# Operand sums of a seven-product down-projection: two of them kept in PSUM, none on GpSimd, five banks for products

## The chip, the cores and the metric

One core of one Trainium2 chip runs the whole program. The metric is the time of one execution in microseconds (us) on the device, as the median of several executions. The engines are TensorE (PE, its weight loads PEld), VectorE (DVE), ScalarE (ACT), GpSimd (POOL) and SyncE (SP, which issues the DMAs).

## The reference

A decoder block of 1024 tokens and width 1024: two token mixers, a layer norm, a convolved gated MLP, a layer norm, a gated embedding and a last norm. The part that is changed is the down-projection of the MLP:

```python
h = causal_dwconv(x @ w_up[i], conv_w[i], conv_b[i])
h_gate, h_val = jnp.split(h, 2, axis=-1)
ffn = (jax.nn.silu(h_gate) * h_val) @ w_down[i]          # (1024 x 2816) @ (2816 x 1024)
x = layer_norm(DEEPNORM_ALPHA * x + ffn, ln2_g[i], ln2_b[i])
```

All is in float32. The kernel splits each float32 operand into a high part (rounded to the multiplier's format) and a low part (what is left), and multiplies high by high, high by low and low by high.

## The kernel before

The first 18 of the 22 row blocks of w_down (each 128 rows) are multiplied in a two-by-two block scheme with seven products in place of eight (the last four blocks follow in a plain scheme and are not touched). The work has three chunks of K (c = 0, 1, 2, six row blocks each), two column groups (cb) and two token groups (gi): twelve **steps**, in the order of `todo` (line 1164), numbered 0 to 11 here. A step is one call of `down` (line 1127): 7 products of 18 matmuls of 128x256, 126 in all, gathered in three PSUM banks: A takes products 0 and 4, B takes 1, 3 and 5, Dk takes 2 and 6. Sums on VectorE (tiles `um`) combine the banks, and four sums per step add the results to the residual `res_all` (a multiply-add by ALPHA when c is 0, line 1159; else a sum, line 1161 by `sums`, line 164).

What the products need is prepared by two functions. `wd_sets(c, cb)` (line 1114) reads 768 columns of w_down per partition into a tile `dr` (one buffer), makes the four combinations in place in it, and writes seven operands `wu` (7 buffers, one full set). `act_sets(c, gi)` (line 1098) does it for the activations, in two halves `a` of 384 columns each, from tiles `ar` (3 buffers, read back from the scratch tensor d_act) into seven operands `au` (13 buffers, two sets of seven less one). Each operand's high part is written by ScalarE (`hi_of`, line 99) and its low part by VectorE or GpSimd (`lo_of`, line 105). The strings AE, BE, SE and TE (line 1125) say which of the two does a low part (AE, BE) and a sum (SE, TE). So a weight set is 4 sums and 7 low parts of 128x768 on VectorE (3 and 5 of them) and GpSimd (1 and 2); an activation set is 8 sums and 14 low parts of 128x384 on VectorE (6 and 7) and GpSimd (2 and 7). A weight set and an activation set together are called a **pair** here; the stage has six pairs.

Before step i, `prepare` emits the sets that step i+1 needs. The order on each engine is then set by a scheduler, so an emission order is not an engine's order. A wu buffer is written again only when the matmuls of two steps have read it, and an au buffer when its steps have.

PSUM has eight banks in this stage (`psum_banks(c1, "f", ch=8)`, line 1095), all for the products: they rotate, so steps i and i+1 have three each and step i+2 two.

At the stage's start the previous stage (up-projection and convolution) still has one block to finish on VectorE, ScalarE and GpSimd (`last_conv`, line 1171, tile `cv`); its result is stored to d_act, and the residual is loaded behind that store, since it lies where those tiles lay (lines 1172 to 1183).

Of the kernel before, what the change touches and what calls it, by code (L numbers as in the profile page):

```python
# [13 lines left out]
ALU = mybir.AluOpType  # L14
# [3 lines left out]
P = 128  # L18
# [12 lines left out]
ALPHA = 2.0 ** 0.25  # L31
# [9 lines left out]
def hybrid_block(ctx: ExitStack, tc: tile.TileContext, x, p, w_in, w_gate_up, b_gate, g_gla, w_gla,  # L41
# [5 lines left out]
    x, p, out = x[0], p[0, 0], out[0]  # L47
# [18 lines left out]
    def psum_banks(stack, tag, **kw):  # L66
        for name, bufs in kw.items():
            PS[name] = pool(f"ps_{tag}_{name}", bufs, PSUM, stack)
# [21 lines left out]
    def nm(s):  # L90
        uid[0] += 1
        return f"{s}_{uid[0]}"
# [15 lines left out]
    def split(hi, lo, src, eh="A", el="V"):  # L108
        hi_of(hi, src, eh)
        lo_of(lo, src, hi, el)  # L110
# [103 lines left out]

    def quad(a):
        return a.rearrange("p (a b) -> p a b", b=P)

    def transpose_in(dst, t, src):

# [755 lines left out]
    with ExitStack() as c1:  # L975
# [101 lines left out]
        late = []  # L1077
# [14 lines left out]
        return (upool if tag == "au" else wpool).tile([P, 2, 768], F32R, name=nm(tag), tag=tag, bufs=bufs)  # L1092

    with ExitStack() as c1:
        psum_banks(c1, "f", ch=8)
        dpl = pool("dwork", stack=c1)

        def act_sets(c, gi):
            U = [unit() for _ in range(7)]
            vw = [u.rearrange("p x (k a q) -> p x k a q", k=3, a=2) for u in U]  # L1100
            acts[c, gi] = vw
            steps = []
            for a in range(2):
                raw = rawp.tile([P, 6, 256], F32, name=nm("ar"), tag="ar", bufs=3)
                t0 = (4 * gi + 2 * a) * P
                loads[0] = nc.sync.dma_start(raw, d_act[c][:, :, t0:t0 + 256])
                q = raw.rearrange("p (h k) (g q) -> p h g k q", h=2, g=2)

                def put(j, src, a=a):
                    split(vw[j][:, 0, :, a], vw[j][:, 1, :, a], src, "A", AE[a][j])  # L1110
                steps.append(left_operands(q[:, 0, 0], q[:, 1, 0], q[:, 0, 1], q[:, 1, 1], put, SE))
            return [lambda x=x, y=y: (x(), y()) for x, y in zip(*steps)]

        def wd_sets(c, cb):
            raw = rawp.tile([P, 6, 2, 256], F32, name=nm("dr"), tag="dr")
            for i in range(2):
                nc.sync.dma_start(raw[:, :, i], wdown_v[:, 6 * c:6 * c + 6, i * HALF + cb * 256:i * HALF + cb * 256 + 256])
            q = raw.rearrange("p (h k) g c -> p h g k c", h=2)
            U = [unit("wu", 7) for _ in range(7)]
            vw = [u.rearrange("p x (k c) -> p x k c", k=3) for u in U]  # L1120
            ws[c, cb] = vw
            return right_operands(q[:, 0, 0], q[:, 0, 1], q[:, 1, 0], q[:, 1, 1],
                                  lambda j, src: split(vw[j][:, 0], vw[j][:, 1], src, "A", BE[j]), TE)

        AE, BE, SE, TE = ('VGVGVGV', 'GVGVGVG'), 'VVGVVGV', 'VVGV', 'VVGV'

        def down(act, W, c, cb, gi):
            A, B, Dk = (bank("ch", (P, 2, 256)) for _ in range(3))
            cols = [slice(i * HALF + cb * 256, i * HALF + cb * 256 + 256) for i in range(2)]

            def prod(ps, j, start):
                for a in range(2):
                    for k in range(3):
                        for n, (x, y) in enumerate(((0, 0), (0, 1), (1, 0))):
                            mm(ps[:, a], act[j][:, x, k, a], W[j][:, y, k], start and a == k == n == 0,
                               k == n == 2, True)

            def tmp():
                return dpl.tile([P, 2, 256], F32, name=nm("um"), tag="um", bufs=4)
            prod(A, 0, True)  # L1140
            s1 = tmp()
            S.activation(s1, A, AF.Copy)
            prod(B, 1, True)
            u2 = tmp()
            sums(u2, s1, B, ALU.add)
            prod(Dk, 2, True)
            prod(B, 3, False)
            u3 = tmp()
            sums(u3, s1, B, ALU.add)
            sums(u3, u3, Dk, ALU.add)  # L1150
            prod(A, 4, False)
            prod(B, 5, False)
            prod(Dk, 6, False)
            sums(s1, s1, B, ALU.add)
            sums(u2, u2, Dk, ALU.add)
            for g, i, src, e in ((1, 1, u3, "V"), (0, 0, A, "V"), (1, 0, s1, "V"), (0, 1, u2, "V")):
                rv = resv[:, gi, :, g, cols[i]]
                if c == 0:
                    V.scalar_tensor_tensor(rv, rv, ALPHA, src, ALU.mult, ALU.add)
                else:  # L1160
                    sums(rv, rv, src, ALU.add, e)

        loads = [None]
        todo = [(c, cb, gi) for c in range(3) for cb in range(2) for gi in range(2)]
# [12 lines left out]
        for i, (c, cb, gi) in enumerate(todo):  # L1177
            if i + 1 < len(todo):
                prepare(*todo[i + 1])
            if i == 0:  # L1180
                with tc.issue_after(loads[0].ins):
                    for t in range(NT):
                        nc.sync.dma_start(RS["res"][t], d_x1[t])
            down(acts[c, gi], ws[c, cb], c, cb, gi)

    def act_plain(i):
        raw = wp.tile([P, 1024], F32, name=nm("wr"), tag="wr", bufs=2)
# [143 lines left out]
```

## Time and profile before

| what | value |
|---|---|
| median of 3 executions | 2160.23 us (2158.56 to 2161.76) |
| profiled execution, its own time | 2157.95 us |
| its span in the profile | 2156.2 us |
| the down-projection's seven-product stage in it | 1735.7 to 1963.5 us, 227.8 us |

The profile shows one execution. "Busy" is the time in which an engine ran an instruction; the granted clock (PEclk) is TensorE's clock as a share of full speed. In rows of the timeline, instructions of the same kind that follow each other are merged: start, length, engine, line, operation, tiles, shape, count, and in brackets the idle time before and who ended it.

### The profile page before, as it was taken

The page shows a single profiled execution, that of the slowest core. Times are in us where ns is not written, and L with a number is a line of the kernel's source. Part 1 is how long each engine was busy: PE and PEld are TensorE (multiplying, and loading weights), DVE is VectorE, ACT ScalarE, POOL GpSimd, SP SyncE. Part 2 cuts the span into 40 slices and gives each one's busy share as a digit, 9 for nine tenths or more (in the row PEclk, how much of TensorE's full clock was granted, in tenths as well). Part 3 has the DMA queues.
Part 4 walks back from the last instruction along what each step waited for, and adds up shares of the span by engine and source line. Part 5 has one row for each costly group of instructions (what it writes and reads, how often), then busy time and mean ns, then how long its engine had stood idle before and what let it go on. Part 6 is the DMA issues. An engine that isn't in the chain of part 4 may idle for free.

```text
span 2156.2 us, 32472 instructions
## 1 busy us (share of the span) xinstructions
PE 2067.9 (96%) x12210; PEld 1815.2 (84%) x12210; DVE 1585.9 (74%) x2700; ACT 841.9 (39%) x1498; POOL 996.8 (46%) x808
## 2 busy tenths in 40 slices
PE   9999999999999999999999979999999978989997
PEld 8888899998988888887788977877777768989897
DVE  3489999999227888786234587777777789986965
ACT  4343312213126766675222244434443444332421
POOL 2432443634431121213332676767767765444743
PEclk9999999999999999999999989999999989999999
DMA  4222211211226776779666351222222134223222
GB/s 137 79 64 79 86 33 55 62 45 52 74 77 126 140 153 133 141 160 227 209 198 148 129 173 49 88 79 78 79 79 88 55 124 150 89 93 118 89 98 79
DMA packets 377566, 227.14 MB, mean 105 GB/s; under 512 B 189328, under 2 KB 351760, under 8 KB 377408
## 3 DMA queue, kind: packets, MB, share of 16 engines
q1 hardware_dynamic: 377408, 225.06, 38.3%
q8 instruction: 96, 1.57, 0.3%
q14 instruction: 62, 0.51, 0.1%
HBM read 146.37 MB, written 40.89 MB: 87 GB/s over the span
## 4 chain that ended last, share of the span: by engine, by line
PE 22%; DVE 12%; POOL 8%; issue 7%; DMA 2%; ACT 2%; SPq 0%; POOLq 0%; DVEq 0%; ACTq 0%
PE mm L155 12%; PE ch L155 10%; POOL wl L106 5%; DVE au L106 2%; DVE cv L1064 1%; DVE wu L106 1%; DVE um L164 1%; DVE h L1020 1%; DVE dr L164 1%; DMA wr<-d_ob 1%; DVE ar L164 1%; ACT cv L1062 1%; DVE res_all L164 1%; POOL lnmv L212 1%; DMA dr<-in_w_down_dram 1%
## 5 line engine op out<-in xcount | busy, mean ns | idle before, releaser
L106 POOL TENSOR_TENSOR wl<-wr,wh 128x512 fp32r<-128x512 f32 x304 | 439.9, 1460 | 287.3 <-ACT wh L101 279.7
L155 PE MATMUL ch<-xs,wh 128*128 128x512 f32 x1232 | 384.8, 394 | 6.7 <-ACT wh L101 4.1
L155 PE MATMUL mm<-Ah,wh 128*128 128x512 f32 x832 | 331.6, 399 | 2.2 <-ACT wh L101 1.3
L155 PE MATMUL mm<-Al,wh 128*128 128x512 f32 x832 | 330.1, 397 | 0.3 <-POOL Al L106 0.3
L155 PE MATMUL mm<-Ah,wl 128*128 128x512 f32 x832 | 329.3, 396 | 0.0
L155 PEld LDWEIGHTS ch<-xs,wh 128*128 128x128 f32 x1232 | 231.7, 189 | 59.4 <-ACT wh L101 4.6
L103 POOL TENSOR_SCALAR wh<-wr 128x512 fp32r<-128x512 f32 x112 | 76.9, 690 | 383.2 <-PE mm L155 199.8
L155 PE MATMUL ch<-xs,wl 128*128 128x512 f32 x616 | 242.4, 394 | 6.6 <-POOL wl L106 6.5
L155 PE MATMUL ch<-wu,au 128*128 128x256 f32 x1512 | 197.1, 294 | 31.2 <-DVE um L164 14.4
L155 PEld LDWEIGHTS ch<-wu,au 128*128 128x128 f32 x1512 | 192.5, 201 | 36.0 <-DVE um L164 14.7
L155 PE MATMUL mm<-wl,Ah 128*128 128x256 f32 x768 | 217.8, 285 | 4.7 <-POOL wl L106 4.6
L155 PE MATMUL mm<-wh,Al 128*128 128x256 f32 x768 | 216.3, 284 | 0.0
L155 PE MATMUL mm<-wh,Ah 128*128 128x256 f32 x768 | 213.8, 284 | 0.0
L1064 DVE SCALAR_TENSOR_TENSOR cv<-h,cw,cv 128x1023 f32<-128x1023 f32 x88 | 167.6, 1905 | 59.9 <-ACT cv L1062 58.4
L101 ACT ACTIVATE wh<-wr 128x512 fp32r<-128x512 f32 (+1 forms) x201 | 120.6, 622 | 186.7 <-PE mm L155 77.0
L155 PEld LDWEIGHTS mm<-Ah,wh 128*128 128x128 f32 x832 | 156.3, 188 | 32.9 <-ACT wh L101 1.8
L155 PEld LDWEIGHTS mm<-Ah,wl 128*128 128x128 f32 x832 | 156.2, 188 | 32.9
L155 PEld LDWEIGHTS mm<-Al,wh 128*128 128x128 f32 x832 | 156.4, 188 | 30.5 <-POOL Al L106 0.8
L651 DVE MATCH_REPLACE8 score<-m,score 128x896 f32<-128x896 f32 (+3 forms) x192 | 166.4, 868 | 0.0
L650 DVE MAX8 m<-score 128x8 f32<-128x896 f32 (+3 forms) x192 | 163.4, 875 | 2.3 <-POOL score L457 2.1
L155 PEld LDWEIGHTS mm<-wl,Ah 128*128 128x128 f32 x768 | 145.8, 190 | 6.4 <-POOL wl L106 5.7
L106 POOL TENSOR_TENSOR wl<-ar,wh 128x512 fp32r<-128x512 f32 x77 | 127.7, 1677 | 44.9 <-ACT wh L101 44.9
(261 smaller groups left out, 4327.0 us busy)
## 6 DMA issues: line engine op xcount, KB each, us to landing
wr<-in_w_in_dram SPq DMA_DIRECT2D x60, 512.0 KB, 3.9
wr<-in_w_up_dram SPq DMA_DIRECT2D x22, 512.0 KB, 3.9
ar<-in_w_up_dram SPq DMA_DIRECT2D x22, 512.0 KB, 3.9
d_act<-cv SPq DMA_DIRECT2D x22, 512.0 KB, 2.6
dr<-in_w_down_dram SPq DMA_DIRECT2D x12, 768.0 KB, 7.1
ar<-d_act SPq DMA_DIRECT2D x12, 768.0 KB, 5.7
d_tg<-tg SPq DMA_DIRECT2D x32, 256.0 KB, 2.0
wr<-in_w_out_dram SPq DMA_DIRECT2D x16, 512.0 KB, 3.6
```

The costliest lines, as they stand in the source:

```text
L101: S.activation(dst, src, AF.Copy, scale=scale)
L103: (V if eng == "V" else G).tensor_scalar(dst, src, scale, 0.0, ALU.mult, ALU.add)
L106: done["GV"[eng != "G"]] = (G if eng == "G" else V).tensor_tensor(out=dst, in0=src, in1=hi.bitcast(F32), op=ALU.subtract)
L155: T.matmul(ps, lhsT=l, rhs=r, start=start, stop=stop, skip_group_check=more)
L164: (G if eng == "G" else V).tensor_tensor(out=out, in0=a, in1=b, op=op)
L212: G.tensor_scalar(dst, src, scale, eps, ALU.mult, ALU.add)
L650: V.max(m8, score[t])
L651: V.match_replace(score[t], m8, score[t], TAKEN)
L1020: V.tensor_tensor(out=out, in0=a, in1=quad(b), op=ALU.add)
L1062: S.activation(o, h, AF.Identity, bias=cbias[:, c:c + 1], scale=cw[:, 2, c:c + 1])
L1064: V.scalar_tensor_tensor(o[:, d:], h[:, :L - d], cw[:, 2 - d, c:c + 1], o[:, d:], ALU.mult, ALU.add)
```

## The change

A new function `bank_sets` takes the place of `left_operands` and `right_operands` in this stage. Of the four combinations of an operand, the first two (s1 = the difference of two blocks, s3 = a third block less s1) are written to two PSUM banks of a new pool `cx` (three banks), and read from there by ScalarE (high part) and VectorE (low part); the other two are still made in place in SBUF. All sums are VectorE's. Of the seven low parts three are VectorE's (the two in PSUM and one more) and four GpSimd's. Weight sets are now cut into two halves of 384 columns, like the activation sets. So each half set has 4 sums and 3 low parts on VectorE and 4 low parts on GpSimd, all of 128x384, and there are 24 half sets.

The products have five banks (`ch=5`) in place of eight. In `down` the sums onto the residual are moved forward, each right behind the product that completes its source, but for the first two steps (`late`), whose residual has not been loaded.

```diff
+    def bank_sets(b, left, put):
+        x, y, z, w, op = ("11", "21", "12", "21", ALU.add) if left else ("12", "11", "21", "12", ALU.subtract)
+        a2 = (b["21"], b["22"]) if left else (b["22"], b["12"])
+        j1, j2, j5, j6 = (3, 2, 5, 6) if left else (2, 3, 6, 5)
+
+        def chain():
+            s1, s3 = (bank("cx", (P, 3, P)) for _ in range(2))
+            sums(s1, b[x], b[y], ALU.subtract)
+            sums(s3, b["22"], s1, ALU.subtract)
+            put(1, s3, "V")
+            sums(b["11"], b[z], s3, ALU.subtract)
+            put(j1, s1, "V")
+
+        def other():
+            sums(b[w], *a2, op)
+            put(j2, b[w], "G")
+        steps = [lambda: put(0, b["11"], "G"), chain, other, lambda: put(4, b[z], "G"),
+                 lambda: put(j5, b["22"], "G"), lambda: put(j6, b["11"], "V")]
+        return steps if left else steps[:4] + steps[:3:-1]
...
-        psum_banks(c1, "f", ch=8)
+        psum_banks(c1, "f", ch=5, cx=3)
...
-                steps.append(left_operands(q[:, 0, 0], q[:, 1, 0], q[:, 0, 1], q[:, 1, 1], put, SE))
+                steps.append(bank_sets({"11": q[:, 0, 0], "12": q[:, 1, 0], "21": q[:, 0, 1], "22": q[:, 1, 1]}, True,
+                                       put))
...
-            return right_operands(q[:, 0, 0], q[:, 0, 1], q[:, 1, 0], q[:, 1, 1],
-                                  lambda j, src: split(vw[j][:, 0], vw[j][:, 1], src, "A", BE[j]), TE)
-
-        AE, BE, SE, TE = ('VGVGVGV', 'GVGVGVG'), 'VVGVVGV', 'VVGV', 'VVGV'
+            steps = []
+            for n in range(2):
+                cs = slice(n * P, (n + 1) * P)
+                def put(j, src, el, cs=cs):
+                    split(vw[j][:, 0, :, cs], vw[j][:, 1, :, cs], src, "A", el)
+                steps.append(bank_sets({"11": q[:, 0, 0, :, cs], "12": q[:, 0, 1, :, cs], "21": q[:, 1, 0, :, cs],
+                                        "22": q[:, 1, 1, :, cs]}, False, put))
...
+            def onto(g, i, src):
+                rv = resv[:, gi, :, g, cols[i]]
+                if c == 0:
+                    V.scalar_tensor_tensor(rv, rv, ALPHA, src, ALU.mult, ALU.add)
+                else:
+                    sums(rv, rv, src, ALU.add)
...
+            if not late:
+                onto(1, 1, u3)
             prod(A, 4, False)
+            if not late:
+                onto(0, 0, A)
             prod(B, 5, False)
+            sums(s1, s1, B, ALU.add)
+            if not late:
+                onto(1, 0, s1)
             prod(Dk, 6, False)
-            sums(s1, s1, B, ALU.add)
             sums(u2, u2, Dk, ALU.add)
-            for g, i, src, e in ((1, 1, u3, "V"), (0, 0, A, "V"), (1, 0, s1, "V"), (0, 1, u2, "V")):
+            for g, i, src in ((1, 1, u3), (0, 0, A), (1, 0, s1))[:3 * late] + ((0, 1, u2),):
+                onto(g, i, src)
...
-            down(acts[c, gi], ws[c, cb], c, cb, gi)
+            down(acts[c, gi], ws[c, cb], c, cb, gi, i < 2)
```

What this does to the order on VectorE is seen where the sets of c = 1 begin, during step 2. Before, from the first low part of its activation set on (dr_2805 is its weight tile, ar_2820 and ar_2821 its activation tiles, um_2802 to um_2804 are step 2's, res_all takes the results):

```order
L106 TENSOR_TENSOR au_2813_16827<-ar_2820_16834,au_2813_16827 128x3x128
L164 TENSOR_TENSOR ar_2821_16836<-ar_2821_16836 128x3x128
L164 TENSOR_TENSOR ar_2820_16834<-ar_2820_16834 128x3x128
L106 TENSOR_TENSOR au_2818_16832<-ar_2821_16836,au_2818_16832 128x3x128
L164 TENSOR_TENSOR ar_2821_16836<-ar_2821_16836 128x3x128
L164 TENSOR_TENSOR ar_2820_16834<-ar_2820_16834 128x3x128
L1159 SCALAR_TENSOR_TENSOR res_all_16307<-res_all_16307,ch_2799_16675 128x2x256
L164 TENSOR_TENSOR um_2804_16754<-um_2802_16696,ch_2800_16676 128x512
```

Now, from the first sum of its weight set on (dr_2821 is the weight tile, cx_2838 to cx_2841 are s1 and s3 of its two halves, um_2818 and um_2819 are step 2's, um_2849 is step 3's):

```order
L164 TENSOR_TENSOR cx_2838_16901<-dr_2821_16872 128x384
L1173 SCALAR_TENSOR_TENSOR res_all_16336<-res_all_16336,um_2818_16751 128x2x256
L164 TENSOR_TENSOR cx_2839_16902<-dr_2821_16872,cx_2838_16901 128x384
L164 TENSOR_TENSOR cx_2840_16910<-dr_2821_16872 128x384
L164 TENSOR_TENSOR dr_2821_16872<-dr_2821_16872 128x3x128
L164 TENSOR_TENSOR um_2819_16771<-um_2819_16771,ch_2817_16732 128x512
L164 TENSOR_TENSOR dr_2821_16872<-dr_2821_16872 128x3x128
L1173 SCALAR_TENSOR_TENSOR res_all_16336<-res_all_16336,um_2819_16771 128x2x256
L164 TENSOR_TENSOR um_2850_17014<-um_2849_16994,ch_2847_16974 128x512
L106 TENSOR_TENSOR wu_2823_16876<-cx_2839_16902,wu_2823_16876 128x3x128
L164 TENSOR_TENSOR dr_2821_16872<-dr_2821_16872,cx_2839_16902 128x3x128
L164 TENSOR_TENSOR cx_2841_16911<-dr_2821_16872,cx_2840_16910 128x384
```

Sums and low parts that read a PSUM tile now stand between those that read SBUF alone, and the preparation of c = 1 begins later among the sums of step 2.

On TensorE, the end of step 0 and the products of step 1 that follow it. Before (ch_2781 is bank Dk of step 0; ch_2793, ch_2794 and ch_2795 are A, B and Dk of step 1):

```order
L155 MATMUL ch_2781_16365<-wu_2759_16231,au_2766_16238 128x256 x6
L155 MATMUL ch_2793_16533<-wu_2753_16225,au_2770_16308 128x256 [waits Pool_49]
L155 MATMUL ch_2793_16533<-wu_2753_16225,au_2770_16308 128x256 x6
L155 MATMUL ch_2794_16534<-wu_2754_16226,au_2771_16309 128x256 [waits PE_49,Activation_49]
L155 MATMUL ch_2794_16534<-wu_2754_16226,au_2771_16309 128x256
L155 MATMUL ch_2795_16535<-wu_2755_16227,au_2772_16310 128x256 [waits PE_49,Activation_49]
```

Now (ch_2793 is Dk of step 0; ch_2810 and ch_2811 are B and Dk of step 1, ch_2815 is A of step 2), with the row on VectorE that frees the bank in the fence behind it:

```order
L155 MATMUL ch_2793_16398<-wu_2759_16234,au_2766_16241 128x256 x17
L155 MATMUL ch_2811_16590<-wu_2755_16230,au_2780_16339 128x256 [waits DVE_49]
L155 MATMUL ch_2811_16590<-wu_2755_16230,au_2780_16339 128x256 x10
L155 MATMUL ch_2811_16590<-wu_2755_16230,au_2780_16339 128x256 [waits Pool_49]
L155 MATMUL ch_2811_16590<-wu_2755_16230,au_2780_16339 128x256 x6
L155 MATMUL ch_2815_16730<-wu_2798_16541,au_2760_16235 128x256 [waits DVE_49]
```

```order
L164 TENSOR_TENSOR um_2795_16437<-um_2795_16437,ch_2793_16398 128x512 [waits PE_49]
L1173 SCALAR_TENSOR_TENSOR res_all_16336<-res_all_16336,ch_2791_16396 128x2x256 [waits DMAHW7_49,DMAHW5_49,DMAHW4_49]
L1173 SCALAR_TENSOR_TENSOR res_all_16336<-res_all_16336,um_2795_16437 128x2x256 [waits DVE_49]
L164 TENSOR_TENSOR um_2813_16629<-um_2812_16609,ch_2810_16589 128x512 [waits DVE_49]
L1173 SCALAR_TENSOR_TENSOR res_all_16336<-res_all_16336,um_2796_16475 128x2x256 [waits DMAHW6_49,DMAHW0_49]
```

Bank Dk of step 1 (ch_2811) waited for operands alone; now it is the bank that A of step 0 (ch_2791) had, and its first matmul stands behind VectorE's sum of ch_2791 onto the residual, which itself waits for the DMAs that load the residual.

## Rows read from the trace of the kernel before

**Rows 1.** The page, part 1: busy time and share of the span by engine.

```profile
PE 2067.9 (96%) x12210; PEld 1815.2 (84%) x12210; DVE 1585.9 (74%) x2700; ACT 841.9 (39%) x1498; POOL 996.8 (46%) x808
```

**Rows 2.** Busy time by stretch of the stage (start:end, length, engines, counts, clock).

```profile
core 0: us, PE busy (x) PEld busy (x) DVE busy (x) ACT busy (x) POOL busy (x), PEclk, DMA share, GB/s
1735.70:1775.30 39.60, 23.92 (x127) 22.05 (x128) 36.72 (x35) 17.10 (x33) 30.01 (x20) 0.74 0.28 93
1775.30:1806.60 31.30, 30.62 (x255) 30.35 (x254) 31.20 (x38) 9.38 (x15) 12.51 (x9) 1.00 0.59 213
1806.60:1829.00 22.40, 17.12 (x129) 16.92 (x128) 22.08 (x27) 10.96 (x21) 13.91 (x11) 0.86 0.31 103
1829.00:1861.90 32.90, 31.53 (x253) 30.68 (x253) 29.55 (x36) 10.76 (x19) 14.52 (x10) 0.99 0.15 49
1861.90:1900.80 38.90, 32.32 (x255) 31.74 (x254) 36.82 (x45) 15.77 (x31) 24.28 (x17) 0.96 0.41 135
1900.80:1963.50 62.70, 61.50 (x506) 60.89 (x506) 50.16 (x63) 17.33 (x28) 23.17 (x15) 1.00 0.29 98
```

**Rows 3.** Timeline of TensorE: one unbroken run, and two that follow a wait.

```profile
1786.92 32.77 PE L155 MATMUL ch<-wu,au 128*128 128x256 f32 x270 [0.68 <-DVE um L164]
1824.97 11.34 PE L155 MATMUL ch<-wu,au 128*128 128x256 f32 x76 [5.28 <-DVE um L164]
1897.21 14.46 PE L155 MATMUL ch<-wu,au 128*128 128x256 f32 x106 [3.65 <-ACT wu L101]
```

**Rows 4.** Groups by shape, 1735:1966 (count | busy us, mean ns | idle before, releasers).

```profile
L106 POOL TENSOR_TENSOR au<-ar,au 128x384 fp32r<-128x384 f32 x42 | 59.1, 1428 | 33.4 <-ACT au L101 33.4
L106 DVE TENSOR_TENSOR au<-ar,au 128x384 fp32r<-128x384 f32 x42 | 41.0, 989 | 0.4 <-ACT au L101 0.3
L106 DVE TENSOR_TENSOR wu<-dr,wu 128x768 fp32r<-128x768 f32 x30 | 37.3, 1248 | 6.2 <-ACT wu L101 6.2
L164 DVE TENSOR_TENSOR ar<-ar 128x384 f32<-128x384 f32 x36 | 30.7, 869 | 0.3
L106 POOL TENSOR_TENSOR wu<-dr,wu 128x768 fp32r<-128x768 f32 x12 | 24.7, 2061 | 23.6 <-ACT wu L101 23.6
L164 POOL TENSOR_TENSOR ar<-ar 128x384 f32<-128x384 f32 x12 | 14.7, 1230 | 7.4 <-DVE ar L164 6.8 <-ACT au L101 0.6
L164 POOL TENSOR_TENSOR dr<-dr 128x768 f32<-128x768 f32 x6 | 11.8, 1973 | 31.4 <-DVE wu L106 18.1 <-DVE dr L164 13.3
L164 DVE TENSOR_TENSOR dr<-dr 128x768 f32<-128x768 f32 x18 | 20.3, 1128 | 0.4 <-DMA dr<-in_w_down_dram 0.3
```

**Rows 5.** Durations (ns, min/median/max) of the tiles um, au, wu, dr.

```profile
L164 DVE TENSOR_TENSOR um<-um,ch x60: 671/675/690, 1761.8 to 1963.6; 128x512 f32<-128x512 f32 x60
L164 DVE TENSOR_TENSOR res_all<-res_all,um x24: 676/691/2302, 1847.6 to 1964.3; 128x512 f32<-128x512 f32 x24
L106 POOL TENSOR_TENSOR au<-ar,au x42: 1002/1340/3251, 1736.2 to 1933.4; 128x384 fp32r<-128x384 f32 x42
L106 DVE TENSOR_TENSOR au<-ar,au x42: 543/781/2203, 1740.0 to 1934.1; 128x384 fp32r<-128x384 f32 x42
L106 DVE TENSOR_TENSOR wu<-dr,wu x30: 943/958/2574, 1734.6 to 1933.2; 128x768 fp32r<-128x768 f32 x30
L164 DVE TENSOR_TENSOR dr<-dr x18: 943/950/1762, 1738.3 to 1935.4; 128x768 f32<-128x768 f32 x18
```

**Rows 6.** Timeline of VectorE, single instructions in a dense stretch.

```profile
1793.27 0.67 DVE L164 TENSOR_TENSOR um<-um,ch 128x512 f32<-128x512 f32 x1
1793.87 0.67 DVE L1159 SCALAR_TENSOR_TENSOR res_all<-res_all,ch 128x512 f32<-128x512 f32 x1
1794.47 0.68 DVE L1159 SCALAR_TENSOR_TENSOR res_all<-res_all,um 128x512 f32<-128x512 f32 x1
1795.07 0.67 DVE L164 TENSOR_TENSOR um<-um,ch 128x512 f32<-128x512 f32 x1
...
1804.52 0.54 DVE L106 TENSOR_TENSOR au<-ar,au 128x384 fp32r<-128x384 f32 x1
1804.99 1.01 DVE L164 TENSOR_TENSOR ar<-ar 128x384 f32<-128x384 f32 x2
```

**Rows 7.** Timeline: last convolution, its store, the residual's loads, the first residual sum.

```profile
1764.03 0.53 SPq L1106 DMA_DIRECT2D ar<-d_act  x1
...
1765.16 2.60 POOL L164 TENSOR_TENSOR cv<-cv,cv 128x1024 f32<-128x1024 f32 x1 [1.16 <-DVE cv L1064]
...
1767.79 0.34 SPq L1074 DMA_DIRECT2D d_act<-cv  x1
1775.27 4.61 SPq L1183 DMA_DIRECT2D res_all<-d_x  x8
1783.58 0.68 DVE L1159 SCALAR_TENSOR_TENSOR res_all<-res_all,ch 128x512 f32<-128x512 f32 x1
```

**Rows 8.** The page, part 6: time from issue to landing.

```profile
d_act<-cv SPq DMA_DIRECT2D x22, 512.0 KB, 2.6
```

More of the change, by code (lines that the diff above doesn't have):

```diff
@@ L1107, in act_sets, with put @@
                 q = raw.rearrange("p (h k) (g q) -> p h g k q", h=2, g=2)
-                def put(j, src, a=a):
-                    split(vw[j][:, 0, :, a], vw[j][:, 1, :, a], src, "A", AE[a][j])
-                steps.append(left_operands(q[:, 0, 0], q[:, 1, 0], q[:, 0, 1], q[:, 1, 1], put, SE))
+                def put(j, src, el, a=a):
+                    split(vw[j][:, 0, :, a], vw[j][:, 1, :, a], src, "A", el)
+                steps.append(bank_sets({"11": q[:, 0, 0], "12": q[:, 1, 0], "21": q[:, 0, 1], "22": q[:, 1, 1]}, True,
+                                       put))
             return [lambda x=x, y=y: (x(), y()) for x, y in zip(*steps)]
@@ L1121, in wd_sets, with down @@
             ws[c, cb] = vw
-            return right_operands(q[:, 0, 0], q[:, 0, 1], q[:, 1, 0], q[:, 1, 1],
-                                  lambda j, src: split(vw[j][:, 0], vw[j][:, 1], src, "A", BE[j]), TE)
-        AE, BE, SE, TE = ('VGVGVGV', 'GVGVGVG'), 'VVGVVGV', 'VVGV', 'VVGV'
-        def down(act, W, c, cb, gi):
+            steps = []
[5 more added lines that the diff above has]
+                                        "22": q[:, 1, 1, :, cs]}, False, put))
+            return [lambda x=x, y=y: (x(), y()) for x, y in zip(*steps)]
+        def down(act, W, c, cb, gi, late):
             A, B, Dk = (bank("ch", (P, 2, 256)) for _ in range(3))
@@ L1150, in down @@
             sums(u3, u3, Dk, ALU.add)
+            if not late:
+                onto(1, 1, u3)
             prod(A, 4, False)
+            if not late:
+                onto(0, 0, A)
             prod(B, 5, False)
+            sums(s1, s1, B, ALU.add)
+            if not late:
+                onto(1, 0, s1)
             prod(Dk, 6, False)
-            sums(s1, s1, B, ALU.add)
             sums(u2, u2, Dk, ALU.add)
-            for g, i, src, e in ((1, 1, u3, "V"), (0, 0, A, "V"), (1, 0, s1, "V"), (0, 1, u2, "V")):
[L1157 to L1161, printed above, removed]
+            for g, i, src in ((1, 1, u3), (0, 0, A), (1, 0, s1))[:3 * late] + ((0, 1, u2),):
+                onto(g, i, src)
         loads = [None]
```

## The prediction

> **What bounds the kernel now.** The page's first part comes first [rows 1]: TensorE is busy for 96% of the span, VectorE for 74%. Over the whole program TensorE is the bound, so a change of this stage can only give back the time in which TensorE stands still in it. The table of stretches says where that is [rows 2]. The stage has 12 x 126 = 1512 matmuls. An unbroken run of 270 takes 32.77 us, 0.121 us each [rows 3], so 1512 of them would take 183.5 us, and the stage takes 227.8: 44 us are lost. Against 0.121 us for each of its matmuls the first stretch loses 24 us of its 39.6, the third 6.8 of 22.4, the fifth 8.0 of 38.9, the fourth 2.3; the second and sixth together lose under 2. Beside that stands VectorE: 36.7 of 39.6, 31.2 of 31.3, 22.1 of 22.4, 29.6 of 32.9, 36.8 of 38.9 us busy [rows 2]. Up to 1900.8 VectorE is the bound wherever TensorE waits, and the long waits end on VectorE's sums and on operands [rows 3]. A wait costs more than its length: after the wait of 5.28 us 76 matmuls took 11.34 us, 0.149 each, some 2.1 us more than in the unbroken run; the granted clock of that stretch is 0.86, a mixture of the two levels, 1.2 and 2.4 GHz, and it is 1.00 where nothing waits [rows 2, 3].
>
> Then what VectorE's time is made of. By groups [rows 4] and by durations [rows 5] there are two kinds of instruction. Those with one operand from PSUM (um<-um,ch) take 671 to 690 ns, all 60 of them. Those with two operands from SBUF are spread: 543 ns to 2203 ns for one form. They are stretched while GpSimd works. Taking 545 ns for 128x384 and 945 ns for 128x768 as undisturbed, the excess is 42 x (989 - 545) = 18.6 us for low parts of activations, 36 x (869 - 545) = 11.7 for their sums, 30 x (1248 - 945) = 9.1 and 18 x (1128 - 945) = 3.3 for the weights [rows 4, 5]. That is 42.7 us over 126 instructions, 0.339 us each.
>
> **The change part by part.**
> *VectorE's plain work stays the same.* Two instructions of 128x512 follow each other by 0.60 us, two of 128x384 by 0.47 [rows 6]; a duration of 945 ns less the same overlap of 0.07 gives 0.87 for 128x768. Preparation before: 78 x 0.47 + 48 x 0.87 = 78.4 us. After: 24 half sets of four sums and three low parts, 168 x 0.47 = 79.0 us. Taking in GpSimd's 18 sums and giving it more low parts cancel.
>
> *What is stretched gets less.* Of the seven instructions of a half set, s3, the sum after it and two low parts read one operand from PSUM; s1, the last sum and the third low part still read two from SBUF: 24 x 3 = 72 against 126. At 0.339 us each that is 24.4 us against 42.7. GpSimd will be busier (next part), by about 15%; so I take 0.39 us, 28.1 us, a saving of 14.6 us over six pairs, 2.4 each (3.0 without the 15%). The bounds: at the weights' sums, 0.183 each, 54 fewer save 9.9; if the activations' low parts, 0.444, are the measure, 24.0.
>
> *A write to PSUM by VectorE* does not occur in the trace. There are 48 now. The nearest rows are the reads: a sum that reads PSUM and one that reads SBUF alone both have a pitch of 0.60 us [rows 6]. I take no cost. As bounds I take 0.1 us for each either way, 4.8 us in all; the shortest durations of the two, 671 and 676 ns, are far closer than that [rows 5]. The trace gives no price for reading PSUM above reading SBUF. The Trainium skill ("Perfetto Trace Analysis", Optimizing Scalar/DVE Operations) does: about 125 ns of access overhead for VectorE on PSUM against 60 on SBUF. By it, 65 ns on 24 x 5 = 120 instructions that now touch PSUM would be an estimated 7.8 us of VectorE, and the gain would shrink to about a half, 2155, next to the rival of no change; the equal pitches speak against it here, and I leave that rival's chance as it stands.
>
> *GpSimd* loses 18 sums and has 24 x 4 = 96 low parts of 128x384 where it had 42, and 12 of 768. They took 1.43 us on average, 1.00 at the shortest [rows 4, 5]. With fewer VectorE instructions to collide with I take 1.3: 125 us, where its low parts and sums were 59.1 + 24.7 + 14.7 + 11.8 = 110 before [rows 4]. A pair has 16, 21 us, and the two steps that cover it last 2 x 126 x 0.121 = 30.5 at least: hidden, and with VectorE's and ScalarE's turns between them I count on that up to about 1.7 us each.
>
> *Five banks.* With eight, a product's bank comes free more than a step before it is wanted; with five, Dk of a step takes the bank that A of the step before left, and stands behind VectorE's sum of that bank onto the residual, four products or 4 x 18 x 0.121 = 8.7 us after it. If VectorE is not that late the wait is nothing; where it is behind already, as at both changes of c, I put down 1 to 2 us in all. What queues behind such a wait on TensorE is every later product.
>
> *The first of these waits* is special: it stands behind the first residual sum, and so behind the residual's loads, which are issued after the last convolution has been stored. Before, GpSimd's product ended at 1765.16 + 2.60, the store was issued, the loads began at 1775.27 and the first sum at 1783.58 [rows 7]. The store took some 7 us, and 2.6 is the usual time [rows 8], since loads issued just ahead of it, at 1764.03, shared the queues [rows 7]. Now, by the order, GpSimd does 22 low parts ahead of its product, 22 x 1.3 = 28.6 us from 1736.2 on [rows 5], about as late as before; if the store then lands in the usual time the first sum comes near 1779, if as before at 1783.6. From there 202 of the first 382 matmuls remain, 24.4 us: 1804 or 1808, against the 1806.6 at which the same count is reached now [rows 2]. I take -2 for the first two stretches, within -3 and +2.
>
> *The sum.* First two stretches -2. The third and fourth, one pair with its change of c: 2.4 to 3.0 of stretched work, and the 2.1 us of slower clock behind the wait, -5. The fifth, the same, -4.5. The sixth, which loses nearly nothing: 0. Banks and a later GpSimd +1.5. Together -10: 2157.95 - 10 = 2148 as the profiled execution, which lies 2.3 under the median of 2160.23; on the median's footing 2150.
>
> **The rivals.**
> *More gain, 2140.* The stretching almost disappears, since GpSimd's own low parts no longer find VectorE on SBUF most of the time, and both changes of c are met without a wait: 6.8 + 2.3 + 8.0 given back less a remainder of 2, and 5 of the first stretch: -20. For it: the bimodal durations, whose lower mode is an undisturbed instruction [rows 5]. Against it: 72 instructions still collide.
>
> *No change, 2160.* The gain is on VectorE, but TensorE waits for banks in place of operands: VectorE's sums onto the residual, now forward in the order, and PSUM's tiles of s1 and s3 (three, two for a half set, so a new half set waits for the low parts of the last) put back what the collisions gave. For it: at the changes of c VectorE has no idle time [rows 2] and 8.7 us of slack are a third of what eight banks gave. Against it: twelve steps fit their sums in outside of the changes of c. A rule of the Trainium skill ("Perfetto Trace Analysis", Matmul Optimizations) stands on this side, that all eight banks should serve the matmuls; here that would cost the waits just described.
>
> *Slower, 2168: the third bank at the start.* Decided by GpSimd's mean for a low part. At 1.3 us the 22 before the product are no later than now; from about 1.65 us on they are: 22 x 1.68 = 37 us puts the product's end near 1776, and the first residual sum, 11 to 16 us behind it as worked out above, near 1789.6; with 24.4 us of matmuls behind that the mark of 1806.6 is reached at 1814, +7.5, and GpSimd at 16 x 1.68 = 27 us for a pair eats the later gain. For it: GpSimd's durations reach 3251 ns [rows 5] and every one of its operands is still SBUF's. Against it: its partner touches SBUF twice over less often.
>
> That the change does not do what it says is out: the order on VectorE has the PSUM tiles in it, and TensorE's third bank has its new wait.
>
> **How the numbers follow.** Forecast 2150 (own range 2145 to 2156): 0.42. More gain, 2140: 0.20. No change, 2160: 0.19. Slower, 2168: 0.19. About 0.2%, 4.3 us, is what a measurement of this kernel can tell from no change; the forecast and the larger gain are beyond it, so faster 0.61 (0.01 of the forecast falls inside), same 0.20, slower 0.19. For the range the low end takes in the larger gain but for its farther half, 2138, and the high end the near part of the slower case, 2166.
>
> **What would show it.** Right: the um, wu and au rows that read a cx tile at about 0.54 us with no spread, the remaining two-SBUF rows still spread; VectorE's busy time of the stage down by some 15 us; the waits before the third and fifth stretches shorter, TensorE's clock nearer 1.00 there; GpSimd's low parts at 1.2 to 1.4 us. Wrong: writes to cx longer than 0.6 us; VectorE's time down but TensorE's long waits now on sums of res_all (the banks); the first wait for the residual's loads ending after 1784; GpSimd's mean over 1.6 us. What I could have wrong above all is where the scheduler puts the forward sums among the preparation, and how far that delays the residual's store.

## The result, and the profile after

| | before | changed |
|---|---|---|
| median | 2159.39 us (2157.45 to 2161.76, 4 runs) | 2147.14 us (2144.47 to 2150.26, 4 runs) |
| profiled execution, its own time (its span) | 2157.95 (2156.2) us | 2145.27 (2143.6) us |
| the stage in that execution | 227.8 us | 217.0 us |

The ratio is 0.9944, with a 95% interval of 0.9932 to 0.9957: 12.2 us faster, where 10 had been forecast. Of the profiled executions' 12.6 us of span, 10.8 lie in the stage. It begins 0.8 us later than before, and what follows it is 2.6 us shorter; that remainder was between 190.0 and 192.8 us in the twelve kernels below, which do not differ there, and was not looked into.

The page's first part (compare [rows 1]) shows 21 us less of VectorE's time, and 3 us more of GpSimd's:

```profile
PE 2063.3 (96%) x12210; PEld 1811.3 (84%) x12210; DVE 1564.6 (73%) x2742; ACT 846.0 (39%) x1540; POOL 1000.0 (47%) x832
```

Busy time of the changed kernel by stretch: steps 0 to 2, 3 to 5, 6 to 8 and 9 to 11; the sum is the whole stage (columns as in [rows 2]). A step is counted here as 126 matmuls, since the scheduler mixes the products of neighbouring steps:

```profile
1736.50:1801.90 65.40, 51.99 (x380) 50.23 (x380) 58.43 (x84) 27.58 (x60) 43.91 (x35) 0.87 0.49 168
1801.90:1853.70 51.80, 47.97 (x380) 47.04 (x379) 49.03 (x80) 23.91 (x54) 32.07 (x28) 0.97 0.21 66
1853.70:1907.10 53.40, 48.16 (x380) 47.59 (x379) 44.56 (x66) 21.99 (x49) 31.39 (x28) 0.94 0.40 130
1907.10:1953.40 46.30, 46.30 (x389) 46.30 (x388) 36.86 (x55) 13.23 (x26) 14.57 (x12) 1.00 0.31 103
sum 216.90, PE 194.42 PEld 191.17 DVE 188.88 ACT 86.71 POOL 121.94; mean PE 48.61 PEld 47.79 DVE 47.22 ACT 21.68 POOL 30.48
```

VectorE's 188.9 us stand against 206.5, the sum of its column in [rows 2]. Steps 0 to 2 took 70.9 us before (1735.7 to 1806.6) and take 65.4 now; steps 3 to 5 55.3 and 51.8. The rest took 101.6 and takes 99.8, up to 1953.5. The last three steps run without a pause at the full granted clock.

Step 0 alone, and step 4, in which the sets of c = 1 are first used:

```profile
1736.50:1770.60 34.10, 21.48 (x128) 19.92 (x128) 34.03 (x49) 19.60 (x43) 31.55 (x25) 0.75 0.28 93
...
1817.60:1838.60 21.00, 17.57 (x129) 16.83 (x129) 20.44 (x29) 10.80 (x27) 19.01 (x17) 0.92 0.47 151
```

The groups of VectorE and GpSimd, by shape (columns as in [rows 4]):

```profile
L106 POOL TENSOR_TENSOR au<-ar,au 128x384 fp32r<-128x384 f32 x48 | 58.5, 1244 | 11.8 <-ACT au L101 11.7
L106 POOL TENSOR_TENSOR wu<-dr,wu 128x384 fp32r<-128x384 f32 x48 | 56.6, 1200 | 68.1 <-ACT wu L101 56.5 <-DVE dr L164 11.6
...
L164 DVE TENSOR_TENSOR res_all<-res_all,um 128x512 f32<-128x512 f32 x24 | 21.4, 890 | 0.3
L106 DVE TENSOR_TENSOR wu<-cx,wu 128x384 fp32r<-128x384 f32 x24 | 13.2, 549 | 0.8 <-ACT wu L101 0.6
L164 DVE TENSOR_TENSOR ar<-ar 128x384 f32<-128x384 f32 x12 | 13.2, 1096 | 0.0
L106 DVE TENSOR_TENSOR au<-cx,au 128x384 fp32r<-128x384 f32 x24 | 13.0, 545 | 0.6 <-ACT au L101 0.6
L1173 DVE SCALAR_TENSOR_TENSOR res_all<-res_all,um 128x512 f32<-128x512 f32 x12 | 12.1, 1011 | 0.1
L106 DVE TENSOR_TENSOR wu<-dr,wu 128x384 fp32r<-128x384 f32 x12 | 11.4, 954 | 0.0
...
L164 DVE TENSOR_TENSOR cx<-ar 128x384 f32<-128x384 f32 x12 | 10.8, 904 | 0.0
L164 DVE TENSOR_TENSOR cx<-dr 128x384 f32<-128x384 f32 x12 | 10.5, 872 | 4.5 <-DMA dr<-in_w_down_dram 4.5
...
L164 DVE TENSOR_TENSOR dr<-dr 128x384 f32<-128x384 f32 x12 | 9.1, 768 | 0.0
L106 DVE TENSOR_TENSOR au<-ar,au 128x384 fp32r<-128x384 f32 x12 | 8.5, 721 | 0.0
...
L164 DVE TENSOR_TENSOR cx<-dr,cx 128x384 f32<-128x384 f32 x12 | 6.6, 553 | 0.1
L164 DVE TENSOR_TENSOR cx<-ar,cx 128x384 f32<-128x384 f32 x12 | 6.6, 549 | 0.0
...
L164 DVE TENSOR_TENSOR ar<-ar,cx 128x384 f32<-128x384 f32 x12 | 6.5, 538 | 0.0
```

On VectorE the two kinds stand apart in one table: whatever reads a cx tile takes 538 to 553 ns on average, and whatever reads two operands from SBUF takes 721 to 1096 for the same shape. The rows cx<-dr,cx and cx<-ar,cx also write PSUM, and do so at no extra price; the rows cx<-dr and cx<-ar write PSUM too, but read two operands from SBUF, and are stretched like the others.

TensorE's timeline shows where it still waits:

```profile
1749.74 11.96 PE L155 MATMUL ch<-wu,au 128*128 128x256 f32 x74 [6.49 <-ACT au L101]
1764.91 20.96 PE L155 MATMUL ch<-wu,au 128*128 128x256 f32 x160 [3.22 <-POOL au L106]
...
1829.22 5.10 PE L155 MATMUL ch<-wu,au 128*128 128x256 f32 x27 [2.47 <-DVE au L106]
...
1897.02 51.33 PE L155 MATMUL ch<-wu,au 128*128 128x256 f32 x408 [4.46 <-DVE au L106]
```

The long waits at the changes of c are now for operands (au); before, the longest one was for a sum on the products' side, um [rows 3]. They also sit in steps 4 and 8, a step later than before.

### The profile page after: what moved, and what is told of

Read it like the earlier page. It is cut to its first block, busy times and chain, and to the rows that moved or that the text cites. A ratio compares the mean times of both kernels' runs of the same rounds, so it can differ in the third digit from the quotient of the medians.

```text
span 2143.6 us, 32563 instructions
## 1 busy us (share of the span) xinstructions
PE 2063.3 (96%) x12210; PEld 1811.3 (84%) x12210; DVE 1564.6 (73%) x2742; ACT 846.0 (39%) x1540; POOL 1000.0 (47%) x832
## 4 chain that ended last, share of the span: by engine, by line
PE 29%; DVE 9%; POOL 7%; issue 5%; DMA 3%; ACT 2%; SPq 0%; POOLq 0%; DVEq 0%; ACTq 0%
PE ch L155 16%; PE mm L155 13%; POOL wl L106 4%; DVE cv L1087 1%; DMA wr<-d_ob 1%; DVE cx L164 1%; DMA dr<-in_w_down_dram 1%; DVE h L1043 1%; ACT cv L1085 1%; DVE ar L164 1%; DVE wu L106 1%; DVE res_all L910 1%; DVE res_all L164 0%; DVE stats L933 0%; POOL lnmv L212 0%
## 5 line engine op out<-in xcount | busy, mean ns | idle before, releaser
L155 PE MATMUL ch<-wu,au 128*128 128x256 f32 x1512 | 194.0, 292 | 22.5 <-DVE au L106 7.2
L155 PEld LDWEIGHTS ch<-xs,wl 128*128 128x128 f32 x616 | 116.5, 189 | 38.2 <-POOL wl L106 14.0
```

Of the source, the lines that this page charges most:

```text
L155: T.matmul(ps, lhsT=l, rhs=r, start=start, stop=stop, skip_group_check=more)
```

## The experiments

Each was timed against the kernel before on the same chip. The forecasts quoted were written before each run.

**1. The same kernel, its two sums in SBUF.**

```diff
-            s1, s3 = (bank("cx", (P, 3, P)) for _ in range(2))
+            s1, s3 = (PS["dw"].tile([P, 3, P], F32, name=nm("cx"), tag="cx", bufs=3) for _ in range(2))
```

> The changed kernel, but the three tiles for s1 and s3 lie in SBUF instead of PSUM; counts of instructions, halves and the five banks stay. Theory (collisions on SBUF): 96 more of VectorE's instructions read two operands from SBUF; at some 0.34 us each VectorE has up to 33 us more to do, and the time goes back by 12 to 25 us, to 2159 to 2172. First rival (the gain is from the half sets and from taking GpSimd out of the sums): within 3 us of 2147.

Measured: 2166.39 us, ratio 1.0036 (1.0024 to 1.0049), as the theory had it. The three tiles' place is worth 19 us, more than the whole change. Its stage (the columns of [rows 2]) and three groups that are undisturbed when they lie in PSUM:

```profile
1736.50:1973.20 236.70, 201.47 (x1523) 196.54 (x1523) 214.87 (x284) 88.94 (x189) 132.28 (x101) 0.91 0.33 111
```

```profile
L106 DVE TENSOR_TENSOR au<-cx,au 128x384 fp32r<-128x384 f32 x24 | 25.0, 1055 | 0.0
...
L164 DVE TENSOR_TENSOR ar<-ar,cx 128x384 f32<-128x384 f32 x12 | 9.9, 821 | 0.0
L164 DVE TENSOR_TENSOR cx<-ar,cx 128x384 f32<-128x384 f32 x12 | 9.0, 746 | 0.0
```

538 to 549 ns became 746 to 1055, and VectorE is busy for 26 us more with the same number of instructions. The excess over 545 ns summed over the instructions open to it is 49.1 us for 168 here and 24.5 for 72 in the changed kernel. Nearly all of it lies in three steps: by the starts of the matmuls in the two traces step 0 takes 41.7 us here and 34.1 in the changed kernel, step 4 28.7 and 20.9, step 8 25.8 and 21.9. Two things besides VectorE's operands differ. ScalarE's 48 high parts of these tiles take 519 to 521 ns here, and 488 to 489 from PSUM, some 1.5 us in all; and the scheduler's order is not quite the same (about one in twenty of VectorE's instructions stands elsewhere). So the place of the tiles is nearly, not wholly, the one difference.

**2. The kernel before, with five banks.**

```diff
-        psum_banks(c1, "f", ch=8)
+        psum_banks(c1, "f", ch=5)
```

> The kernel before with five banks for products instead of eight and nothing else. Theory: five banks cost 1 to 2 us, 2160 to 2162. Rival (the banks are what holds the gain down): slower by 5 us or more. Rival (fewer banks make an order that is better for VectorE): faster by 3 us or more.

Measured: 2159.4 us, ratio 1.0003 (0.9994 to 1.0012), neither rival. Five banks cost nothing that can be told from zero; the 1 to 2 us of the theory are not excluded.

**3. The kernel before, GpSimd's sums on VectorE.**

```diff
-        AE, BE, SE, TE = ('VGVGVGV', 'GVGVGVG'), 'VVGVVGV', 'VVGV', 'VVGV'
+        AE, BE, SE, TE = ('VGVGVGV', 'GVGVGVG'), 'VVGVVGV', 'VVVV', 'VVVV'
```

> The kernel before with GpSimd's 18 sums given to VectorE and nothing else. Theory (VectorE is the bound): 12 x 0.47 + 6 x 0.87 = 10.9 us more for VectorE, less some collisions saved; slower by 2 to 8 us, 2161 to 2167. Rival (what hurt was the chain from VectorE through GpSimd's sums and back): faster by 4 us or more, 2155 or less.

Measured: 2149.87 us, ratio 0.9960 (0.9948 to 0.9973), 8.8 us faster: the rival, and the theory's sign was wrong. The stage, and then what ScalarE waited for (total us, times, longest), first of the kernel before and then of this one:

```profile
1735.70:1954.70 219.00, 194.90 (x1514) 190.12 (x1515) 206.32 (x257) 82.50 (x145) 93.56 (x59) 0.95 0.35 117
```

```profile
ACT wu L101 <- POOL dr L164: 30.0, 6, 6.3
ACT au L101 <- DVE ar L164: 24.4, 7, 5.4
...
ACT au L101 <- POOL ar L164: 17.6, 6, 5.8
...
ACT wu L101 <- DVE dr L164: 10.6, 4, 4.9
```

```profile
ACT au L101 <- DVE ar L164: 36.5, 14, 6.0
ACT wu L101 <- DVE dr L164: 30.8, 10, 5.2
```

VectorE is busy as long as before, 206.3 against 206.5 us, though it makes 18 more sums: the 10.9 us of plain work are offset, for the most part, by 8.9 us less stretching (33.8 of excess against 42.7). The stage is 8.8 us shorter all the same. ScalarE's wait for sums, 82.6 us over the four rows, fell to 67.3. So VectorE's busy time alone did not set the stage. Each GpSimd sum, the third of four, stood inside the chain from sum to high part to low part to product, and the fourth sum reads its result; that this is the cause is argued from these waits.

**4 and 5. GpSimd's low parts replaced by writes.** Both write zeros in place of GpSimd's 96 low parts, so the low parts of four operands in seven are missing in the result. The second writes them three times, to keep GpSimd busy. Of each edit only the helper's line is shown; in `bank_sets` the `"G"` of the four low parts becomes `"M"`.

```diff
-        lo_of(lo, src, hi, el)
+        G.memset(lo.bitcast(F32), 0.0) if el == "M" else lo_of(lo, src, hi, el)
```

```diff
-        lo_of(lo, src, hi, el)
+        [G.memset(lo.bitcast(F32), 0.0) for _ in range(3)] if el == "M" else lo_of(lo, src, hi, el)
```

> The changed kernel, but GpSimd writes zeros instead of its 96 low parts, so that it reads no SBUF there (these low parts are left out of the result). Theory: the 72 instructions that are still stretched, 0.34 us each, shrink to their undisturbed 0.54 us, 24 us less for VectorE, and TensorE's waits at the changes of c nearly vanish: 2130 to 2138. Rival (buffers that come free late bound the changes of c): 2143 to 2147.

> As the run with zeros in place of GpSimd's 96 low parts (those low parts are left out of the result), but each is written three times, so that GpSimd is about as busy as in the changed kernel (3 x 0.42 = 1.26 us each against 1.22) and still reads no SBUF. Theory (collisions are what costs): VectorE's two-SBUF instructions stay at 0.54 us, and the time is 2122 to 2128. Rival (GpSimd's length itself sets the waits at the start and at the changes of c): 2138 to 2147.

Measured: 2122.22 us, ratio 0.9833 (0.9820 to 0.9847), and 2127.25 us, ratio 0.9853 (0.9840 to 0.9867). The first is 8 us below the range of its theory, the second within it. The stages of the two, and a group of the second:

```profile
1734.80:1928.50 193.70, 185.64 (x1523) 184.88 (x1523) 156.48 (x284) 85.95 (x189) 42.09 (x95) 0.97 0.41 135
```

```profile
1738.60:1935.60 197.00, 186.98 (x1522) 185.12 (x1522) 158.06 (x284) 85.73 (x189) 109.75 (x287) 0.97 0.41 133
```

```profile
L106 DVE TENSOR_TENSOR wu<-dr,wu 128x384 fp32r<-128x384 f32 x12 | 6.6, 553 | 0.2 <-ACT wu L101 0.2
```

GpSimd at 109.8 us of work that reads no SBUF stretches hardly anything (954 ns became 553; 3.0 us of excess over 72 instructions, against 24.5), and the stage is 20 us shorter. At 42.1 us it is only 3.3 shorter still. So GpSimd's time itself hardly keeps the stage above 197. But the zeros differ from the low parts in a second way: they read no operand, so they wait for no sum and no high part. What TensorE waited for GpSimd's low parts in the changed kernel (total us, times, longest):

```profile
PE ch L155 <- POOL au L106: 4.8, 3, 3.2
...
PE ch L155 <- POOL wu L106: 2.0, 1, 2.0
```

That is 6.8 us, against 1.2 in the second of these, so some 6 of the 20 us may be this wait, and not the collision; no run parts the two here. Experiment 1, where every low part keeps its operands, is the cleaner evidence for the collision. The Trainium skill ("SBUF — State Buffer", section "SBUF: two separate sides") describes a port pair shared by the two engines, taken for a whole instruction, by VectorE's instructions with two SBUF inputs against GpSimd's that read SBUF. The rows agree on both conditions: one operand from PSUM, or a GpSimd that only writes, and the stretching is gone but for 0.04 us an instruction.

**6. Six banks for products, two for the tiles.** The edit is `ch=6, cx=2` for `ch=5, cx=3`.

> The changed kernel with six banks for products and two for s1 and s3. Theory (banks are a small matter either way): within 2 us of 2147. Rival (the five banks' waits on VectorE's sums are what is left): faster by 3 us or more. Rival (a half set has to wait for the two tiles of the last): slower by 3 us or more.

Measured: 2146.59 us, ratio 0.9944 (0.9930 to 0.9958): the same as the changed kernel, and the theory.

**7. The third sum in PSUM too.**

```diff
-            s1, s3 = (bank("cx", (P, 3, P)) for _ in range(2))
+            s1, s3, s6 = (bank("cx", (P, 3, P)) for _ in range(3))
...
-            sums(b["11"], b[z], s3, ALU.subtract)
+            sums(s6, b[z], s3, ALU.subtract)
+            put(j6, s6, "V")
```

> The changed kernel with the third sum of each half set in PSUM too (three tiles, five banks for products as now), its low part right behind it. Theory: 24 fewer of VectorE's instructions are open to collisions, 8 us less for VectorE, faster by 2 to 5 us: 2142 to 2145. Rival (the three tiles now hold a half set back until the last one has been read): 2147 to 2155.

Measured: 2142.69 us, ratio 0.9926 (0.9914 to 0.9939), 4.4 us below the changed kernel's median, within the theory's range; the two intervals overlap by a little, so the gain is likely, not certain. VectorE is busy for 13.6 us less than in the changed kernel, of which the time shows a third (the stage, columns as in [rows 2]):

```profile
1738.30:1952.50 214.20, 195.99 (x1523) 191.84 (x1523) 175.26 (x284) 86.94 (x189) 115.24 (x101) 0.94 0.36 122
```

**8. Three low parts of a half set on GpSimd.** The edit is `put(j2, b[w], "V")` for `"G"`.

> The changed kernel with the low part of the fourth sum on VectorE: three of a half set's low parts on GpSimd, four on VectorE. VectorE has 24 x 0.47 = 11 us more plain work and, with a quarter less of GpSimd's, some 8 us less stretching of the 96 instructions that are open to it. Theory (collisions cost as much as work): within 4 us of 2147, rather faster since GpSimd is 29 us shorter at the changes of c. Rival (VectorE's count of instructions is the bound): slower by 5 us or more.

Measured: 2153.5 us, ratio 0.9975 (0.9965 to 0.9984): slower than the changed kernel by 6.4 us, the rival. VectorE has 9 us more to do and GpSimd 29 less, and the stage is 5.9 longer. The theory counted on less stretching, and there is more: 30.5 us of excess over the 96 open instructions, 0.32 each, against 24.5 over 72, 0.34 each. A quarter less of GpSimd hardly changed what one open instruction pays (columns as in [rows 2]):

```profile
1740.40:1963.30 222.90, 199.30 (x1523) 193.13 (x1523) 197.97 (x308) 87.01 (x189) 93.19 (x77) 0.93 0.35 117
```

**9. The kernel before, sums on VectorE, and the new split of low parts.**

```diff
-        AE, BE, SE, TE = ('VGVGVGV', 'GVGVGVG'), 'VVGVVGV', 'VVGV', 'VVGV'
+        AE, BE, SE, TE = ('GVGVGGV', 'GVGVGGV'), 'GVVGGVG', 'VVVV', 'VVVV'
```

> The kernel before (whole weight sets, eight banks, all in SBUF) with every sum on VectorE, as in the run that gave 2149.9, and now also with the changed kernel's split of the low parts, four of seven on GpSimd. It lies between that run and the changed kernel with its tiles in SBUF (2166.4), which differs from it by the half sets and the banks. Theory (GpSimd's larger share makes the collisions that PSUM then spares): 2160 to 2167. Rival (the half weight sets cost it): 2147 to 2153.

Measured: 2160.48 us, ratio 1.0010 (1.0001 to 1.0019): the theory. Against experiment 3 GpSimd's larger share costs 10.6 us: VectorE does 18 low parts less, and is still busy for 3.6 us more, since its excess went from 33.8 to 48.6 us. Its stage (columns as in [rows 2]):

```profile
1737.20:1966.40 229.20, 197.51 (x1514) 193.01 (x1515) 209.87 (x240) 82.06 (x145) 118.59 (x77) 0.93 0.34 112
```

**10. The changed kernel, with the fourth sum on GpSimd.** The edit is `sums(b[w], *a2, op, "G")`.

> The changed kernel with the fourth sum of each half set on GpSimd. VectorE has 24 x (0.47 + 0.34) = 19 us less, GpSimd some 29 us more, which it spends between VectorE's raw operand and its own low part. Theory (as the kernel before showed when its sums were taken from GpSimd: a sum there is a loss, by its collisions and its length at the changes of c): slower by 3 to 10 us, 2150 to 2157. Rival (VectorE's time is all that counts): faster by 4 us or more.

Measured: 2143.79 us, ratio 0.9933 (0.9920 to 0.9945), 3.3 us below the changed kernel's median with overlapping intervals: not slower, which the theory had said, and less than the rival's 4. A sum on GpSimd is not bad as such. This one feeds one operand, whose low part is GpSimd's own, and no further sum; the one of the kernel before fed the next sum. That the place in the chain makes the difference fits both, but no run moved one sum alone between the two places.

**11. Three sums in PSUM, with four tiles and four banks.** The edit is `ch=4, cx=4` in the kernel of experiment 7.

> The run with the third sum in PSUM too (2142.7), with four tiles for sums and four banks for products instead of three and five. Theory (banks matter little while each product has one when it starts): within 3 us of 2142.7. Rival (four banks put products behind VectorE's sums): slower by 4 us or more.

Measured: 2143.25 us, ratio 0.9929 (0.9917 to 0.9942): as experiment 7, and the theory. Even four banks for products are enough.

**12. Experiments 7 and 10 together.**

> Both edits that were faster than the changed kernel together: the third sum in PSUM (2142.7) and the fourth sum on GpSimd (2143.8); three tiles, five banks for products. Of VectorE's preparation only s1, 24 instructions, still reads two operands from SBUF. Theory (VectorE's time, with its collisions, bounds the start and the changes of c): the two gains add at least in part, 2138 to 2142. Rival (GpSimd, at some 145 us of the stage's 215 and all of the changes of c, is the bound now): 2143 to 2150.

Measured: 2145.15 us, ratio 0.9940 (0.9926 to 0.9954): the rival, as far as the time goes. The two gains don't add. The stage, and the waits of this kernel:

```profile
1735.80:1948.50 212.70, 193.79 (x1521) 189.84 (x1520) 164.15 (x261) 87.11 (x189) 139.41 (x125) 0.94 0.37 123
```

```profile
DVE um L164 <- PE ch L155: 25.8, 19, 4.7
ACT au L101 <- DVE cx L164: 20.0, 14, 4.9
POOL dr L164 <- DVE cx L164: 18.9, 8, 8.2
...
PE ch L155 <- ACT au L101: 10.9, 5, 7.2
```

VectorE is busy for 25 us less than in the changed kernel and waits longer for products itself, 25.8 us against 17.2 there; of TensorE's 18.8 us of waits 10.9 end on ScalarE's high parts, against 6.5 of 22.5 there. That fits a chain that goes from engine to engine, at the start (step 0 still takes 30.9 us) and at the changes of c (steps 4 and 8, 20.6 and 21.8), as what is left, and not one engine's time. GpSimd as the bound, which the rival named, is not shown by it, nor excluded.

One part of the change has no run of its own, and needs none: with the sums onto the residual put back behind the last product, the scheduler gives the same order on every engine, in the changed kernel and, the other way round, in the kernel before. Moving them forward moves nothing.

**The path from before to changed.** The medians make a path of four steps: GpSimd's sums to VectorE, 2158.6 to 2149.9 (-8.8); the larger share of low parts on GpSimd, to 2160.5 (+10.6); all that is left but the place of the tiles, to 2166.4 (+5.9); s1 and s3 in PSUM, to 2147.1 (-19.3). The third step is not one cause: it holds the half weight sets, the five banks (0.8 us in experiment 2, -1.3 to 2.6 by its interval), tiles of their own for s1 and s3, which before were made in place over their operands, and another order of an operand's sums and low parts. No run takes these apart.

## Why the prediction held, step by step

*What bounds.* Half right. "VectorE is the bound wherever TensorE waits" is the step that failed: experiment 3 shortened the stage by 8.8 us with VectorE's busy time unchanged, and experiment 12 took 25 us from VectorE for 4.3 of the stage. VectorE's stretching is one cause and the chain through the engines another. The 8.8 us from GpSimd's sums alone were put at nothing ("cancel").

*The collisions.* Right in mechanism, and nearly in size. Counted were 72 open instructions at 0.339 us, 24.4 us, raised to 28.1 for a busier GpSimd; measured were 24.5, that is 0.341 each (the six groups of two-SBUF instructions of the table after, less 545 ns each). The raise did not occur: GpSimd was busy for 121.9 us in the stage against 118.4 before, not 15% more, since its low parts took 1.22 us and not 1.3 (115 us for 96, where 125 were forecast). VectorE's busy time in the stage fell by 17.7 us, close to the 18.2 of the excess (42.7 to 24.5): the plain work stayed the same within 2 to 3 us. One kind was counted on neither side: 36 sums onto the residual (res_all<-res_all,um) read two operands from SBUF too. They average 890 and 1011 ns in the table after, 910 and 1160 before, and 739 and 687 in experiment 5, beside 676 for the shortest [rows 5]; that is some 2 us less stretching.

*What the sum left out.* Terms were missing on both sides, and that is why 10 came near 12; so far the near hit is luck. The forecast gave 9.5 us to fewer collisions with the clock behind the waits, and 2 to the residual's earlier loads; on the path above the tiles in PSUM give 19.3 and GpSimd's sums 8.8, and the larger share of low parts with the rest of the change takes 16.5 back.

*Writes to PSUM.* Right: no cost (553 and 549 ns for s3, of dr and of ar). The Trainium skill's larger overhead for VectorE on PSUM ("Perfetto Trace Analysis", Optimizing Scalar/DVE Operations) does not show: the low parts that read PSUM take 545 and 549 ns, the shortest that read SBUF took 543 [rows 5].

*Banks.* The cost of 1 to 2 us was small enough, but the mechanism was wrong. The first residual sum was forecast near 1779, and came there; but the bank that was said to wait for it did not. Its row in VectorE's timeline, and one ahead of it:

```profile
1775.16 0.68 DVE L164 TENSOR_TENSOR um<-um,ch 128x512 f32<-128x512 f32 x1
...
1779.74 0.69 DVE L1173 SCALAR_TENSOR_TENSOR res_all<-res_all,ch 128x512 f32<-128x512 f32 x1 [1.77 <-DMA res_all<-d_x]
```

TensorE's run from 1764.91 to 1785.87, above, has 92 matmuls of the stage ahead of it; the first of Dk of step 1 is the 181st, and it began at 1777.1, before that sum. It cannot have stood behind the sum of bank A, as the text on the order above says of ch_2811. By the places that the built kernel gives its banks, ch_2811 has that of ch_2792, bank B of step 0, whose last sum is the row at 1775.16; the bank of ch_2791 went to B of step 2. The banks do not simply come round in turn, and an order of instructions without the banks' places does not tell which sum frees which. In the changed kernel TensorE waited for um sums for 2.0 us in all, in the kernel before for 14.4 (first the changed kernel):

```profile
PE ch L155 <- DVE um L164: 2.0, 3, 0.8
```

```profile
PE ch L155 <- DVE um L164: 14.4, 9, 5.3
```

With six, five and four banks the time stays where it was (experiments 2, 6, 11). The Trainium skill's rule that all eight banks should serve the matmuls ("Perfetto Trace Analysis", Matmul Optimizations) has no price here that can be told from zero; it stood on the side of the rival of no change.

*By stretch.* Forecast were -2 for steps 0 to 2, -5 for steps 3 to 5, -4.5 for the rest and +1.5 for banks and a later GpSimd; measured were -5.5, -3.5 and -1.8. The sum is right to a microsecond, its split is not. The start gained most: step 0 went from 39.5 to 34.1 us, to 30.3 with a third sum in PSUM (experiment 7), and to 27.0 in experiment 5. The -2 were put down to the residual's loads, which come later than step 0; with the tiles in SBUF step 0 takes 41.7 (experiment 1), so the start gains from fewer collisions, which the sum gave to the later stretches alone. At the changes of c the wait did not go; it moved one step on, with VectorE busy for 20.4 of the 21.0 us of step 4 and GpSimd for 19.0.

*The rivals.* More gain did not come: the 72 remaining instructions still collide at full price, and experiments 4 and 5 show what lies there, 20 to 25 us with the shorter waits for GpSimd's low parts in it. The slower case needed GpSimd's low parts above 1.65 us; they took 1.22.

## What to carry to other kernels

Where VectorE and GpSimd both read SBUF, ask of each VectorE instruction whether one of its two operands could stand in PSUM; here that took the same instructions from some 0.8 us (experiment 1) to 0.55. A plan that gives GpSimd more work should be costed with what it does to VectorE's two-operand instructions, and work may be cheaper on VectorE than in the middle of a chain on GpSimd. And a saving on the busiest engine is worth its time only until the chain between the engines shows: 25 us of VectorE were worth 4 of the stage at the end, and 2 of the median. Of the variants that compute the whole result the third sum in PSUM had the lowest median, 2142.69 us, 0.2% below the changed kernel.

## What the runs showed of the hardware

- VectorE's two-operand instructions of 128x384 that read one operand from PSUM run at the undisturbed 0.54 to 0.56 us, whether they write SBUF or PSUM, with GpSimd busy for 42 to 68% of the stage (experiments 8 and 10).
- GpSimd's writes alone (0.42 us for 128x384) stretch VectorE's instructions with two SBUF operands by 0.04 us each (experiment 5); its low parts, which read SBUF, by 0.34 (the changed kernel).
- GpSimd is slower too where VectorE reads more of SBUF: its low part of 128x384 averages 1.33 us in experiment 1, 1.22 in the changed kernel and 1.15 in experiment 7.
- ScalarE's high part of 128x384 takes 0.49 us from PSUM and 0.52 from SBUF (the changed kernel and experiment 1).
